# Hybrid pooling trunk on one core: in the second input phase, S4 of token block 1 formed on the chip from A12 and S2 instead of stored by the first phase and loaded

## The chip, the cores and the metric

The kernel runs on one core of a Trainium2 chip. The metric is the device time of one execution in microseconds (us), lower is better. TensorE is called PE here, VectorE DVE, ScalarE ACT, GpSimd POOL and SyncE SP, as in the profile; L783 is line 783 of the kernel.

## The reference, cut to what matters

With one layer (DEPTH = 1) only the pooling mixer runs, on 4096 tokens of width 1024, all in float32:

```python
normed = rms_norm(x, norm_w)
u, gate = split(normed @ in_w, 2)            # in_w is 1024 x 2048
pooled = trailing means of u over 2/4/8/16 tokens (one width per 256 columns) - u
mixed  = pooled @ group_w (per group of 256) + group_b
y      = mixed * scale * silu(gate)
out    = rms_norm(x + y @ out_w, final_norm_w)
```

## The kernel before, in words

**Three phases of PE work.** The group matrices are folded into the input weights at the start. Then an input phase over the first two pooling groups (kind "a"), a second input phase over the other two (kind "b", which multiplies the same normalised activations with other weights), and an output phase (kind "o"). The input phases go over four blocks of 1024 tokens (b = 0 to 3), the output phase over eight of 512. A step is one product of one block; the list `steps` has 28 + 28 + 56 of them, and the last loop of the kernel runs them in order from the third on: loads up to three steps ahead (`load_reach`, L1695), operands split one or two steps ahead (`split_reach`, L1698), the product (`run`, L1443), its eviction (`evict_in`, L1126).

**Seven products in place of eight.** Each block's activation matrix is cut into quarters A11, A12, A21, A22 (keys "11", "12", "21", "22"; each quarter is two tiles of 128 x 1024, h = 0 and 1), and multiplied in seven products P1 to P7 whose operands are sums of quarters. In the second input phase a block's products run in the order P1, P2, P6, P7, P5, P4, P3. Their operands are A11 for P1, A12 for P2, S2 = A22 - S3 for P6, S3 = A11 - A21 for P7, S1 = A11 + S2 for P5, A22 for P4, and **S4 = A12 - S2 for P3**. A11, A12, S3 and A22 come from DRAM, where the first phase left them (`sd`); S2 and S1 are formed on DVE (`form_in`, L651). S4 can either be formed on DVE (`form_s4`, L761, right after P6's operand is split, in place of A12) or be loaded. STORED (L34) says for which blocks it is stored and loaded; before, that is all four:

```python
elif q and is_stored(i, b):                                    # load_in, L645
    s["11" if i == P5 else "12"] = load_saved(b, i)
...
if i == P6 and (q or b) and not (q and is_stored(P3, b)):      # split_in, L685
    form_s4(b)
if q and is_stored({P1: P5, P2: P3}.get(i), b):                # L687
    for u in s.pop(key):
        give(u)
```

So before, A12 of a block is given back after P2's operand is split, and S4 comes in as two loads of 512 KB issued with P3's load. The first phase forms S4 in any case, for its own P3; it stores it from the ACT queue (L609) when `sd` has a place for it.

**Operands.** A product's operand is split into a high part (ACT, `copy`, L229) and the remainder (DVE, `sub`, L215) in one of four tiles op0 to op3, taken in turn; `mm3` (L778) makes three matmuls of the two parts of both sides. One step of an input phase is 48 matmuls of 128 x 512: 24 that read the first op tile, then 24 that read the second. The first matmul of an op tile reads only its high part, the second matmul reads its low part. P1, P2, P7 and P4 accumulate in banks 0 to 3, the others in banks 4 to 7; the products of one bank set follow each other as in P1, P2, then P6 on the other set, then P7, then P5 on the other, then P4, then P3 on the other.

**Slots.** Tiles of 128 x 1024 are handed out of two pools (11 `st`, 8 `vt`) by `take` (L187), the one longest free first; `give` puts a tile at the end. A tile's next writer waits for its last reader. `keep` (L1735) sets how many `vt` tiles stay reserved.

**What sets the order.** Instructions are written in program order and put on the engines' queues by a list scheduler; each engine and each DMA queue works its own queue in order. All loads and nearly all stores of the second input phase stand on SP's queue, so a transfer that waits for its tile holds back all behind it. In the middle of a block the DVE also does the pooling of the products of the block before (`pool_steps`, L1036: scans L1070, L1092, the product with the gate, and sums of four quarters stored to `sumd`, L1024), and the output weights are prepared in the same stretch (`make_wo`, L440: loads L305, scaling on ACT L320, sums on DVE, stores L340 to L345).

Of the kernel before, what the change touches and what calls it, by code (L numbers as in the profile page):

```python
# [30 lines left out]
FIRST_INNER = 1  # L31
INNER = {2: (1, 7), 4: (2, 6)}
INNER_IN = (0,)
STORED = {3: (0, 1, 2, 3)}  # L34

P1, P2, P3, P4, P5, P6, P7 = range(1, 8)
ORDER_IN = (P1, P2, P6, P7, P5, P4, P3)
# [55 lines left out]
def kernel(  # L93
# [138 lines left out]
    def split(dst, src):  # L232
# [20 lines left out]
        for i in range(P1, P7 + 1)  # L253
# [3 lines left out]
            i: [dram.tile([P, 2, H], F32, name=f"sd{b}_{i}_{h}") for h in range(2)]  # L257
            for i in (P1, P2, P7, P4, *(i for i in STORED if b in STORED[i]))
        }
# [388 lines left out]
    def is_stored(i, b):  # L648
        return b in STORED.get(i, ())

# [1245 lines left out]
```

## Time and profile before

| what | value |
|---|---|
| time, median of 3 runs | 906.63 us (905.44 to 909.16) |
| profiled execution | 905.18 us |
| its span, first to last instruction | 903.4 us |
| mean granted TensorE clock | 0.998 |
| PE busy | 895.7 us, 99% |
| DVE busy | 776.2 us, 86% |
| ACT busy | 487.6 us, 54% |
| DMA packets | 205.40 MB, mean 227 GB/s |
| chain that ended last | PE 98% |

The rows are those of the profiled execution alone; 1.8 us of its time lie outside the span. Busy PE counts overlapping matmuls, so how dense PE is has to be read from the distance between matmuls. The chain that ended last is followed back from the last instruction to what released it.

### The profile page before, as it was taken

How to read it: one execution, taken by the hardware profiler on the slowest of the kernel's cores; microseconds unless marked ns; L12 is line 12 of the kernel's file. 1: busy time of each engine (PE TensorE's matmuls, PEld its weight loads, DVE VectorE, ACT ScalarE, POOL GpSimd, SP SyncE). 2: the span in 40 equal slices, each digit the busy share in tenths (PEclk: the TensorE clock that was granted, in tenths of full speed). 3: DMA queues.
4: the chain of work that ended last, by engine and by line, in shares of the span. 5: the costliest groups of instructions: out<-in, count | busy, mean ns of one | idle time of the engine just before them, and what ended most of it. 6: DMA issues, size and time to landing. Idle time of an engine off the chain costs nothing.

```text
span 903.4 us, 12068 instructions
## 1 busy us (share of the span) xinstructions
PE 895.7 (99%) x4482; PEld 790.3 (87%) x4482; DVE 776.2 (86%) x973; ACT 487.6 (54%) x807; POOL 42.0 (5%) x75
## 2 busy tenths in 40 slices
PE   9999999999999999999999999999999999999997
PEld 7888888888888888898888888888898998999996
DVE  5999994894998998699589589799999989889897
ACT  6979547447346556355445545654446435355354
POOL 0023101101100000000000000000100000000000
PEclk9999999999999999999999999999999999999999
DMA  9986966956856844056826866855875584584652
GB/s 349 408 320 198 347 221 193 316 187 230 335 207 228 280 146 140 24 154 225 326 89 224 331 236 215 291 194 190 278 254 203 188 308 147 180 279 158 216 187 94
DMA packets 75148, 205.40 MB, mean 227 GB/s; under 512 B 6928, under 2 KB 29840, under 8 KB 75088
## 3 DMA queue, kind: packets, MB, share of 16 engines
q1 hardware_dynamic: 67440, 179.17, 56.3%
q10 hardware_dynamic: 5040, 16.79, 5.0%
q0 software_dynamic: 2608, 8.66, 2.7%
q8 instruction: 35, 0.57, 0.3%
q14 instruction: 25, 0.20, 0.1%
HBM read 130.13 MB, written 74.46 MB: 226 GB/s over the span
## 4 chain that ended last, share of the span: by engine, by line
PE 98%; DVE 1%; ACT 0%; issue 0%; DVEq 0%; ACTq 0%
PE bank L783 87%; PE bank L972 6%; PE bank L497 3%; PE bank L816 1%; PE bank L1485 0%; DVE op L215 0%; DVE w L215 0%; DVE st L215 0%; PE bank L563 0%; ACT vt L1303 0%; DVE st L1373 0%; DVE st L1345 0%; ACT vt L1335 0%; ACT vt L229 0%; DVEq L1892 0%
## 5 line engine op out<-in xcount | busy, mean ns | idle before, releaser
L783 PE MATMUL bank<-op,w 128*128 128x512 f32 x2640 | 571.4, 379 | 0.2
L783 PEld LDWEIGHTS bank<-op,w 128*128 128x128 f32 x2640 | 498.4, 189 | 72.3 <-DVE op L215 1.0
L783 PE MATMUL bank<-w,op 128*128 128x512 f32 (+1 forms) x1068 | 232.2, 377 | 0.0
L783 PEld LDWEIGHTS bank<-w,op 128*128 128x128 f32 x1068 | 198.3, 189 | 26.9 <-issue 0.2
L215 DVE TENSOR_TENSOR op<-st,op 128x1024 fp32r<-128x1024 f32 x79 | 95.2, 1209 | 28.5 <-ACT op L229 28.3
L229 ACT ACTIVATE op<-st 128x1024 fp32r<-128x1024 f32 x79 | 82.4, 1048 | 57.5 <-PE bank L783 45.0
L229 ACT ACTIVATE op<-vt 128x1024 fp32r<-128x1024 f32 x69 | 71.8, 1052 | 58.4 <-PE bank L783 32.4
L215 DVE TENSOR_TENSOR op<-vt,op 128x1024 fp32r<-128x1024 f32 x69 | 83.6, 1215 | 10.4 <-ACT op L229 10.3
L229 ACT ACTIVATE vt<-bank 128x512 f32<-128x512 f32 x94 | 53.2, 590 | 44.3 <-PE bank L783 32.5
L229 ACT ACTIVATE bank<-bank 128x512 f32<-128x512 f32 (+1 forms) x76 | 38.0, 502 | 63.4 <-PE bank L783 32.1
L215 DVE TENSOR_TENSOR op<-s_st,op 128x1024 fp32r<-128x1024 f32 x31 | 37.6, 1217 | 12.0 <-ACT op L229 12.0
L229 ACT ACTIVATE op<-s_st 128x1024 fp32r<-128x1024 f32 x31 | 32.4, 1049 | 21.9 <-PE bank L783 11.8
L1373 DVE TENSOR_TENSOR vt<-bank,vt 128x512 f32<-128x512 f32 x56 | 37.9, 680 | 3.3 <-PE bank L783 3.3
L972 PE MATMUL bank<-w,op 128*128 128x256 f32 x288 | 40.0, 275 | 0.0
L972 PEld LDWEIGHTS bank<-w,op 128*128 128x128 f32 x288 | 37.8, 192 | 1.3
L215 DVE TENSOR_TENSOR vt<-bank,vt 128x512 f32<-128x512 f32 x50 | 32.7, 683 | 6.9 <-PE bank L783 6.8
L1237 POOL TENSOR_SCALAR oms<-oss 128x2 f32<-128x2 f32 x14 | 9.8, 696 | 615.4 <-ACT st L1264 443.2
L1070 DVE TENSOR_TENSOR_SCAN vt<-vt,bf 128x512 f32<-128x512 f32 x28 | 34.4, 1267 | 1.3 <-ACT vt L229 1.3
L215 DVE TENSOR_TENSOR w<-st,w 128x1024 fp32r<-128x1024 f32 (+2 forms) x25 | 28.1, 1132 | 8.5 <-ACT w L229 8.5
L229 ACT ACTIVATE w<-st 128x1024 fp32r<-128x1024 f32 (+2 forms) x25 | 24.2, 984 | 18.8 <-DMA st<-wod 9.0
L215 DVE TENSOR_TENSOR vt<-vt,vt 128x1024 f32<-128x1024 f32 (+1 forms) x29 | 33.0, 1140 | 0.1
L229 ACT ACTIVATE st<-bank 128x512 f32<-128x512 f32 x34 | 20.0, 594 | 24.0 <-PE bank L783 16.2
(171 smaller groups left out, 817.9 us busy)
## 6 DMA issues: line engine op xcount, KB each, us to landing
st<-in_x SPq DMA_DIRECT2D x27, 512.0 KB, 5.8
st<-in_xt SPq DMA_DIRECT2D x27, 512.0 KB, 8.9
vt<-in_x SPq DMA_DIRECT2D x27, 512.0 KB, 5.0
sd<-st ACTq DMA_DIRECT2D x27, 512.0 KB, 5.6
vt<-yd SPq DMA_DIRECT2D x18, 512.0 KB, 5.6
st<-sd SPq DMA_DIRECT2D x17, 512.0 KB, 5.4
out<-vt SPq DMA_DIRECT2D x17, 512.0 KB, 3.5
yd<-st SPq DMA_DIRECT2D x16, 512.0 KB, 2.9
```

The costliest lines, as they stand in the source:

```text
L215: made.append(nc.vector.tensor_tensor(out=dst, in0=a, in1=b, op=op))
L229: made.append(nc.scalar.activation(dst, src, func, **how))
L497: latest[0] = nc.tensor.matmul(ps2[kk][:, j * 256 : (j + 1) * 256], a[:, kk, 2 * j + t, :], maps if len(pairs) == 1 else woven(maps), star ...
L783: latest[0] = nc.tensor.matmul(ps, a, b, start=start and n == 0, stop=stop and n == 2, skip_group_check=True).ins
L816: latest[0] = nc.tensor.matmul(quarter_bank(banks_[c], n), a[:, x_, k, c * P : (c + 1) * P], right[:, y_, k], start=start and k + m == 0, ...
L972: latest[0] = nc.tensor.matmul(dst, a[k][x_], b[k][y_], start=start and k + n == 0, stop=k == 1 and n == 2, skip_group_check=True,).ins
L1070: nc.vector.tensor_tensor_scan(s[:, j, at:end], v[:, j, at:end], v[:, j, at - win : end - win], sums_of[j] if sums_of else 0.0, ALU.add, A ...
L1237: nc.gpsimd.tensor_scalar(out=ms, in0=ss, scalar1=-0.5 / D, scalar2=-0.5 * EPS, op0=ALU.mult, op1=ALU.add)
L1373: partial["added"] = nc.vector.tensor_tensor(out=dst, in0=src, in1=dst, op=ALU.add).ins
```

## The change

```diff
-STORED = {3: (0, 1, 2, 3)}
+STORED = {3: (0, 2, 3)}
```

`STORED` has one key, 3, which is P3. Block 1 leaves the list, and three things follow in the program. The first phase has no place in `sd` for block 1's S4, so two stores on the ACT queue go. The second phase issues no load for it, so two loads on SP's queue go. And A12 of block 1 (in tiles vt6 and st2) isn't given back after P2; `form_s4` subtracts S2 from it in place, two DVE instructions, and P3's operand is split from there. As A12's tiles stay taken and the two tiles of the load aren't taken, the tiles that later instructions get are others from there on, and the scheduler's order changes around it. All other instructions are the same, and PE's order is the same row for row. Names in the rows below: st, vt and s_st tiles are slots (st9_98 is slot st9; s9_st1_3058 is slot st1 in its second life, and its last number differs between the two programs only by counting), bank4_73 is bank 4.

**DVE, where block 1's S2 is formed** (S2 in s9_st1 for h = 0 and s10_st7 for h = 1; st9 and st5 hold A11 and become S1; op2 and op3 are P6's operand; op rows are the low parts). Before:

```order
L215 TENSOR_TENSOR s9_st1_3058<-vt7_107,s7_st3_3022 128x1024
L215 TENSOR_TENSOR st9_98<-s9_st1_3058,st9_98 128x1024
L215 TENSOR_TENSOR s10_st7_3059<-vt1_101,s8_st10_3023 128x1024
L215 TENSOR_TENSOR op2_87<-s9_st1_3058,op2_87 128x1024
L215 TENSOR_TENSOR st5_94<-s10_st7_3059,st5_94 128x1024
L215 TENSOR_TENSOR op3_88<-s10_st7_3059,op3_88 128x1024
```

Now:

```order
L215 TENSOR_TENSOR s9_st1_3054<-vt7_107,s7_st3_3018 128x1024
L215 TENSOR_TENSOR vt6_106<-vt6_106,s9_st1_3054 128x1024
L215 TENSOR_TENSOR st9_98<-s9_st1_3054,st9_98 128x1024
L215 TENSOR_TENSOR s10_st7_3055<-vt1_101,s8_st10_3019 128x1024
L215 TENSOR_TENSOR op2_87<-s9_st1_3054,op2_87 128x1024
L215 TENSOR_TENSOR st2_91<-st2_91,s10_st7_3055 128x1024
L215 TENSOR_TENSOR op3_88<-s10_st7_3055,op3_88 128x1024
```

The rows on vt6 and st2 are the new S4. The second of them stands where S1's second half (st5) stood; that row has moved on, to the next place.

**DVE, ahead of P7's operand of block 1** (op0 and op1; st0 and s11_st4 belong to the pooling and its sums). Before:

```order
L215 TENSOR_TENSOR st0_89<-vt3_103,st0_89 128x1024
L215 TENSOR_TENSOR op0_85<-s7_st3_3022,op0_85 128x1024
L215 TENSOR_TENSOR vt2_102<-st6_95,st0_89 128x512
L215 TENSOR_TENSOR op1_86<-s8_st10_3023,op1_86 128x1024
L215 TENSOR_TENSOR vt2_102<-vt2_102,st6_95 128x512
L215 TENSOR_TENSOR s11_st4_3060<-st0_89,vt2_102 128x512
L215 TENSOR_TENSOR op2_87<-st9_98,op2_87 128x1024
```

Now:

```order
L215 TENSOR_TENSOR st0_89<-vt3_103,st0_89 128x1024
L215 TENSOR_TENSOR st5_94<-s10_st7_3055,st5_94 128x1024
L215 TENSOR_TENSOR vt2_102<-st6_95,st0_89 128x512
L215 TENSOR_TENSOR op0_85<-s7_st3_3018,op0_85 128x1024
L215 TENSOR_TENSOR vt2_102<-vt2_102,st6_95 128x512
L215 TENSOR_TENSOR op1_86<-s8_st10_3019,op1_86 128x1024
L215 TENSOR_TENSOR s11_st4_3056<-st0_89,vt2_102 128x512
L215 TENSOR_TENSOR op2_87<-st9_98,op2_87 128x1024
```

Between st0 and op0 there now stand two rows, st5 of 128 x 1024 and the first vt2 of 128 x 512; before, op0 followed st0 directly.

**ACT, evictions of P2 and P6 of block 1** (from banks 0 to 3 and 4 to 7; the L320 rows scale output weights after their loads; op rows are high parts). Before:

```order
L229 ACTIVATE op2_87<-st9_98 128x1024
L229 ACTIVATE vt4_104<-bank4_73 128x512
L229 ACTIVATE vt4_104<-bank5_74 128x512
L320 ACTIVATE s7_st3_3022<-s7_st3_3022,colt_114 128x512 x2
L229 ACTIVATE vt0_100<-bank6_75 128x512
L229 ACTIVATE vt0_100<-bank7_76 128x512
L229 ACTIVATE op3_88<-st5_94 128x1024
```

Now:

```order
L229 ACTIVATE op2_87<-st9_98 128x1024
L320 ACTIVATE s10_st7_3055<-s10_st7_3055,colt_114 128x512 x2
L229 ACTIVATE st6_95<-bank6_75 128x512
L320 ACTIVATE s7_st3_3018<-s7_st3_3018,colt_114 128x512
L229 ACTIVATE st6_95<-bank7_76 128x512
L229 ACTIVATE op3_88<-st5_94 128x1024
L320 ACTIVATE s7_st3_3018<-s7_st3_3018,colt_114 128x512
L229 ACTIVATE s11_st4_3056<-bank4_73 128x512
L229 ACTIVATE s11_st4_3056<-bank5_74 128x512
```

Banks 4 and 5 of P6 are now evicted last of the four, behind two loads' scaling, and into s11_st4, which the pooling's sums leave only when their store to `sumd` has landed; before, they went into vt4, first.

## Prediction

> **What bounds the kernel now.** I read the page's first two parts, then the engines' busy time by stage, then the chain that ended last.
>
> ```profile
> PE 895.7 (99%) x4482; PEld 790.3 (87%) x4482; DVE 776.2 (86%) x973; ACT 487.6 (54%) x807; POOL 42.0 (5%) x75
> ```
>
> By itself 99% says little, since matmuls overlap. The table by stage (time, then PE, weight loads, DVE, ACT, POOL, clock, DMA share, GB/s) and one row of the chain say more:
>
> ```profile
> 60.00:394.00 334.00, 334.00 (x1589) 293.57 (x1588) 281.07 (x306) 194.09 (x297) 24.81 (x43) 1.00 0.61 215
> 394.00:571.00 177.00, 176.98 (x823) 154.71 (x822) 147.17 (x159) 87.95 (x169) 0.00 (x0) 1.00 0.65 236
> 571.00:894.00 323.00, 323.00 (x1741) 289.77 (x1742) 295.51 (x436) 156.53 (x260) 9.75 (x14) 1.00 0.61 210
> ```
>
> ```profile
> 394.49 176.34 PE bank L783 x817
> ```
>
> From 60 to 894 us PE is idle for 0.02 us in all, and 817 matmuls follow each other every 176.34/817 = 0.216 us at a granted clock of 1.00. So PE sets the end, and what the change can take from the time is nothing: it leaves PE's matmuls and their order alone, and there is no wait of PE to shorten in the stretch that it touches. It can only add, by making an operand or a bank late. The question is which cushions it eats.
>
> The Trainium skill ("Perfetto Trace Analysis", section "Identifying the Most-Contended Engine") says that matmul busy time is a poor measure of how near a kernel is to its limit, and that weight-load busy time should be read; by its 87% some 113 us of PE would still be open. The row of 0.216 us speaks against that here: the skill's "TensorE: Matmul & The Clock Gate", Part 1, gives 215.7 ns between matmuls of 512 columns at full clock, which the trace agrees with. By the one rule a removed wait could pay, by the row it can't; I go by the row, and what is left for the other is in the chance of the faster rival.
>
> **What goes.** In the first phase two stores of S4 leave ACT's queue, in the second two loads leave SP's. The first two rows are those stores; of the second two, the first holds one of those loads beside one for block 2, the second is the other load.
>
> ```profile
> 160.72 0.33 ACTq L609 DMA_DIRECT2D sd<-st  x1
> ...
> 162.47 0.33 ACTq L609 DMA_DIRECT2D sd<-st  x1
> ```
>
> ```profile
> 427.76 1.97 SPq L626 DMA_DIRECT2D st<-sd  x2
> ...
> 431.66 0.32 SPq L626 DMA_DIRECT2D s_st<-sd  x1
> ```
>
> That is 2 x 0.33 us of issuing on ACT at 161 to 163 us, some 1.3 us on SP, and four transfers of 0.52 MB out of 205 MB. PE hides them all: it is busy for 334.00 of 334 us around the stores and did not wait for S4's loads either. I cost them at 0. If PE did not cover them, the removed issues would be worth 0.7 us on ACT and 1.3 us on SP at the most.
>
> **What comes.** Two DVE subtractions of 128 x 1024. DVE around block 1's P6 and P7 (start, duration, form; a bracket is idle time ahead and its releaser):
>
> ```profile
> 404.69 1.22 DVE L215 TENSOR_TENSOR s_st<-vt,s_st 128x1024 f32<-128x1024 f32 x1
> 405.94 1.23 DVE L215 TENSOR_TENSOR st<-s_st,st 128x1024 f32<-128x1024 f32 x1
> 408.69 1.23 DVE L215 TENSOR_TENSOR s_st<-vt,s_st 128x1024 f32<-128x1024 f32 x1 [1.52 <-DMA vt<-sd]
> 409.83 1.22 DVE L215 TENSOR_TENSOR op<-s_st,op 128x1024 fp32r<-128x1024 f32 x1
> 410.96 1.22 DVE L215 TENSOR_TENSOR st<-s_st,st 128x1024 f32<-128x1024 f32 x1
> 412.10 1.22 DVE L215 TENSOR_TENSOR op<-s_st,op 128x1024 fp32r<-128x1024 f32 x1
> 413.23 3.63 DVE L1070 TENSOR_TENSOR_SCAN vt<-vt,bf 128x512 f32<-128x512 f32 x3
> ...
> 421.95 1.21 DVE L215 TENSOR_TENSOR st<-vt,st 128x1024 f32<-128x1024 f32 x1
> 423.08 1.21 DVE L215 TENSOR_TENSOR op<-s_st,op 128x1024 fp32r<-128x1024 f32 x1
> 424.22 0.68 DVE L215 TENSOR_TENSOR vt<-st,st 128x512 f32<-128x512 f32 x1
> 424.82 1.21 DVE L215 TENSOR_TENSOR op<-s_st,op 128x1024 fp32r<-128x1024 f32 x1
> 425.96 0.68 DVE L215 TENSOR_TENSOR vt<-vt,st 128x512 f32<-128x512 f32 x1
> 426.67 0.69 DVE L215 TENSOR_TENSOR s_st<-st,vt 128x512 f32<-128x512 f32 x1
> ```
>
> Starts in a dense run lie 1.14 us apart after a row of 1024 and 0.60 after one of 512, since neighbours overlap by 0.08. The first subtraction (vt6) falls behind the row at 404.69, into the idle 1.52 us that waits for A22's second load: it costs 1.14 to 1.25 us of DVE and nothing of the time. If that load landed earlier, the cover would shrink, but then everything behind it would start earlier by as much.
>
> The second (st2) takes the place of S1's second half (the row at 410.96), so everything from 412.10 to 421.95 stays where it is. S1's half is what moves: with the first vt2 row it now stands ahead of op0's low part. **The term of the sum** is there: op0 moves from 423.08 to 423.08 + 1.14 + 0.60 = 424.82, and is done at 424.82 + 1.21 = 426.03 in place of 424.29.
>
> When does PE want it? P1 of block 1 starts at 394.33, and P1, P2 and P6 are 144 matmuls:
>
> ```profile
> 394.33 31.25 PE L783 MATMUL bank<-op,w 128*128 128x512 f32 x144
> ```
>
> 144 x 0.2158 = 31.08, so P7's first matmul starts at 425.41, and its second, the first to read the low part, at 425.63. Before, op0 was ready 1.34 us ahead of that. Now it is 0.40 late, and with 0.05 us for the wait's end (0.02 to 0.1 lie between releases and starts in these rows) **PE stands still for about 0.45 us**. It is dense afterwards, so the end moves by that. Bounds: 0 if A22's load lands 0.4 us earlier, since the first subtraction leaves the DVE free at 408.30; 1.3 + 0.45 if the scheduling around st0 slips by another row of 1024 (estimate from the rows above).
>
> Queued behind op0 on DVE are op1, done at 424.82 + 1.14 + 0.60 + 1.21 = 427.77 while PE wants its low part at 425.63 + 24 x 0.2158 = 430.81, and P5's op2, done near 429.5 and wanted at 435.99. Both have 3 us and more left, and S1's moved half is wanted later still, as P5's second operand at 441. P3's operand no longer waits for a load: S4 is there from 412 us, wanted at 456.
>
> **The evictions** change more than the DVE. ACT, and SP with landing times in this stretch (KB, median us from issue to landing):
>
> ```profile
> 421.93 0.59 ACT L229 ACTIVATE vt<-bank 128x512 f32<-128x512 f32 x1
> ...
> 428.04 1.33 ACT L320 ACTIVATE s_st<-s_st,colt 128x512 f32<-128x512 f32 x2 [4.42 <-DMA s_st<-in_out_w]
> 429.28 1.06 ACT L229 ACTIVATE vt<-bank 128x512 f32<-128x512 f32 x2
> 430.23 1.05 ACT L229 ACTIVATE op<-st 128x1024 fp32r<-128x1024 f32 x1
> ```
>
> ```profile
> s_st<-in_out_w SPq DMA_DIRECT2D x4, 512.0 KB, 3.7
> st<-sd SPq DMA_DIRECT2D x4, 512.0 KB, 6.1
> ...
> sumd<-s_st SPq DMA_DIRECT2D x1, 512.0 KB, 4.3
> ```
>
> Bank 4, which P5 overwrites, was evicted at 421.93. Now ACT first needs the weight load into s10, which waits for S1's moved half: issued 424.3, landed 424.3 + 3.7 = 428.0, scaled by 429.3, bank 6 by 429.8. The load into s7 follows op0: 426.03 + 3.7 = 429.7, first scaling 430.5, bank 7 431.0, op3 432.0, second scaling 432.6. Bank 4 goes into s11, whose store is issued after DVE's sum: op1 done 427.77, sum 428.4, store landed 428.4 + 4.3 = 432.7. So bank 4 is out at 433.3. P5 starts at 394.33 + 192 x 0.2158 + 0.45 = 436.2. The cushion falls from 13.3 to 2.9 us and holds; I cost it at 0. With 6.1 us for each of these transfers, the longest median above, bank 4 is out at 435.7, still in time.
>
> Farther on, block 2's P2 and P6 keep their DVE work in another order, with their low parts no later than before, and from block 3 on the rows stand in the same order as before, but for single rows of 512 or 1024 with over 3 us left. Cost 0.
>
> **Sum:** 905.18 (profiled) + 0.45 = 905.63 for the profiled execution. That execution lies 1.45 us under the median of the runs, 906.63, so the median after should be **907.1 us**.
>
> **The rivals.**
> - Hidden altogether: A22's load, which fixes the dense run on DVE, lands 0.4 us earlier, and op0 is in time. The loads ahead of it on SP are the same, which speaks against it. 906.6.
> - Faster: 2.1 MB less on the DMA queues and two loads fewer in front of block 2's take a wait away. PE's 0.02 us of idle time in 834 speaks against any gain; 906.6 at best, and over 0.5% less only if the runs scatter.
> - Slower, by the late eviction of bank 4: ACT stands in line behind the load into s10, issued 11 us later than before, so each us by which that landing passes 3.7 + 2.9 = 6.6 us holds P5 up by one. At twice the longest median, 12.2 us, P5 would wait 5.6 us and the kernel would take 907.1 + 5.6 = 912.7. Against it: medians of 3.7 for these loads, and two fewer loads beside them.
>
> On that rival the Trainium skill ("TensorE: Matmul & The Clock Gate", section on HAM oscillation) adds that a PE gap over about 3.4 us halves the clock for the next window. A gap of 5.6 us would then cost about 1.7 us more (an estimate from that page's window), 914.4, one of 0.45 us nothing; no row between 60 and 894 us shows such a gap, and the clock there is 1.00.
>
> - That the change does not do what it says is excluded by the order: the two rows are there, the four transfers are not.
>
> **How the numbers follow.** The forecast has a chance of 0.75, hidden 0.12, the late eviction 0.10 (over 0.5% in 0.04), faster 0.03. About 0.5%, 4.5 us, is what a measurement of this kernel can tell from no change. So faster 0.02, within 0.92, slower 0.06 (the two hundredths beyond the eviction are scatter). The three runs of before lie from 1.2 under to 2.5 over their median. The range takes the hidden case less that scatter, 905.4, and the forecast plus it, 909.6; an eviction late by up to 2.5 us falls within it.
>
> **What would show it.** In the profile after: DVE's idle time ahead of S2's second half down from 1.52 to under 0.5 us; op0's low part near 426.0; a PE wait for DVE's op of 0.4 to 0.5 us near 425.6; bank 4's eviction near 433 and no wait of PE for ACT there; 203.3 MB in place of 205.4. A PE wait for an eviction near 436, or a second one in block 2, would make the prediction wrong.

## The result, and the profile after

| | before | after |
|---|---|---|
| median of 14 runs each | 905.46 us (904.90 to 909.16) | 909.22 us (905.96 to 911.70) |
| ratio after to before, 95% interval | | 1.0029 (1.0018 to 1.0040) |
| profiled execution | 905.18 us | 910.07 us |
| its span | 903.4 us | 908.3 us |
| DMA packets | 205.40 MB | 203.30 MB |

The medians lie 3.76 us apart; by the ratio the change costs about 2.6 us (0.0029 x 905.46). That is within the bound of 0.5% and within the range given, but the sum had only 0.45 us. The runs of after come in lumps: four of 14 lie between 905.96 and 906.19, within 0.3 us of what the forecast's one term gives on this median (905.46 + 0.45); the other ten lie at 907.45 and above. So the question is what the others pay for.

Two stages of the profile after, to be read against the table quoted in the prediction (the first stage, 60 to 394 us, is full as before; time, PE, weight loads, DVE, ACT, POOL, clock, DMA share, GB/s):

```profile
394.00:571.00 177.00, 176.43 (x820) 154.21 (x819) 146.96 (x156) 86.27 (x166) 0.00 (x0) 1.00 0.62 224
571.00:894.00 323.00, 320.32 (x1720) 286.79 (x1719) 295.47 (x429) 155.47 (x257) 9.58 (x14) 0.99 0.62 213
```

Before, PE was idle for 0.02 us between 60 and 894. Now it is idle for 0.57 in the middle stretch and 2.68 in the last, where the clock also reads 0.99. Each stretch has a single gap. PE's rows of the profile after, with the idle time ahead and its releaser:

```profile
426.26 6.09 PE L783 MATMUL bank<-op,w 128*128 128x512 f32 x27 [0.57 <-DVE op L215]
...
574.25 9.08 PE L783 MATMUL bank<-op,w 128*128 128x512 f32 x33 [2.68 <-DVE op L215]
```

The first is the wait that was forecast, ahead of P7 of block 1. The second is ahead of P7 of **block 3**, two blocks behind the last instruction that the change adds. Finer stretches of the same table, directly behind the second gap:

```profile
574.30:575.50 1.20, 1.20 (x4) 0.97 (x5) 1.20 (x2) 0.00 (x0) 0.00 (x0) 0.60 0.99 314
575.50:579.00 3.50, 3.50 (x12) 2.87 (x11) 1.57 (x2) 0.00 (x0) 0.00 (x0) 0.65 0.97 315
```

PE ran there at a granted clock below 1.00 and lost 0.40 x 1.20 + 0.35 x 3.50 = 1.7 us, as much as 3.4 us at half speed would. The two gaps and this loss, 0.57 + 2.68 + 1.7 = 4.95, account for the span's 4.9 us.

DVE's rows of after that answer to those of the prediction, and two of block 3:

```profile
408.85 1.23 DVE L215 TENSOR_TENSOR s_st<-vt,s_st 128x1024 f32<-128x1024 f32 x1 [0.66 <-DMA vt<-sd]
...
424.99 1.22 DVE L215 TENSOR_TENSOR op<-s_st,op 128x1024 fp32r<-128x1024 f32 x1
...
550.95 1.22 DVE L215 TENSOR_TENSOR s_st<-s_st,vt 128x1024 f32<-128x1024 f32 x1
...
572.98 1.22 DVE L215 TENSOR_TENSOR op<-vt,op 128x1024 fp32r<-128x1024 f32 x1
```

The first two are S2's second half of block 1 and op0's low part, done at 426.21 where 426.03 was forecast. The last two are the same two instructions in block 3. Before, they stood here:

```profile
549.32 1.22 DVE L215 TENSOR_TENSOR st<-s_st,s_st 128x1024 f32<-128x1024 f32 x1
...
569.58 1.22 DVE L215 TENSOR_TENSOR op<-s_st,op 128x1024 fp32r<-128x1024 f32 x1
```

They are 1.63 and 3.40 us later in after, while PE by itself would be 0.57 later. PE had nothing to spare there even before. These are its weight load for P7's second matmul in block 3, the first to read that operand's low part, and then the matmul ahead of it and that matmul:

```profile
570.85 0.19 PEld L783 LDWEIGHTS bank<-op,w 128*128 128x128 f32 x1 [0.42 <-DVE op L215]
```

```profile
570.45 0.38 PE L783 MATMUL bank<-op,w 128*128 128x512 f32 x1
570.85 0.48 PE L783 MATMUL bank<-op,w 128*128 128x512 f32 x1
```

The two start 0.40 us apart and not 0.216, so PE had already lost 0.18 us. A matmul's row lasts 0.38 us, so a delay of up to 0.38 - 0.216 = 0.16 us leaves no idle time; what is left of this one is the 0.02 us that the prediction quotes as PE's whole idle time. The row of the chain quoted there, 394.49 with 176.34 us, ends at 570.83, at this place.

Why the two rows are later shows in the chain of work that ended last. Before it was 98% PE; in after it leaves PE at 494.98 and comes back to it at 574.25 (start, duration, what):

```profile
494.98 0.52 ACT s_st L229
495.50 6.13 DMA s_st<-in_out_w
...
504.45 1.24 DVE op L215
505.70 3.96 DMA s_st<-in_out_w
...
520.78 4.90 DMA s_st<-wod
...
549.08 7.19 DMA st<-wod
...
573.06 1.15 DVE op L215
```

This is a **side chain** of 79 us beside PE: the output weights of `make_wo` are loaded (L305), scaled, summed, stored and loaded again, and DVE does the pooling and P7's operand behind them in order. SP's rows of before for its stations:

```profile
497.93 0.38 SPq L305 DMA_DIRECT2D s_st<-in_out_w  x1
498.40 0.86 SPq L305 DMA_DIRECT2D st<-in_out_w  x2
...
517.74 0.44 SPq L428 DMA_DIRECT2D s_st<-wod  x1
...
545.30 0.32 SPq L1024 DMA_DIRECT2D sumd<-st  x1
...
547.46 0.38 SPq L451 DMA_DIRECT2D st<-wod  x1
```

Before, the last of block 2's weight loads was issued by 499.26, and the reload at 517.74. In after the last load gets a tile that op1's subtraction reads until 505.69, so it is issued at 505.70, the reload at 520.78, and the load at 549.08 instead of 547.46. The question for the experiments was what makes this chain late: the two DVE rows, the other tiles, or the transfers themselves.

### The profile page after: what moved, and what is told of

It is laid out like the page before. It is cut to its first block, busy times and chain, and to the rows that moved or that the text cites. A ratio compares the mean times of both kernels' runs of the same rounds, so it can differ in the third digit from the quotient of the medians.

```text
span 908.3 us, 12064 instructions
## 1 busy us (share of the span) xinstructions
PE 897.3 (99%) x4482; PEld 791.3 (87%) x4482; DVE 779.7 (86%) x975; ACT 487.5 (54%) x807; POOL 41.8 (5%) x75
## 2 busy tenths in 40 slices
DMA packets 74572, 203.30 MB, mean 224 GB/s; under 512 B 6864, under 2 KB 29776, under 8 KB 74512
## 4 chain that ended last, share of the span: by engine, by line
PE 87%; DVE 7%; DMA 3%; issue 2%; ACT 1%; SPq 0%; DVEq 0%; ACTq 0%
PE bank L783 77%; PE bank L972 6%; PE bank L497 3%; DVE vt L1070 2%; DVE op L215 1%; DVE st L215 1%; DMA s_st<-in_out_w 1%; PE bank L816 1%; DVE s_st L215 1%; DMA st<-wod 1%; DVE vt L1092 1%; DMA s_st<-wod 1%; DVE w L215 1%; DMA early<-in_wut 0%; DVE vt L215 0%
## 5 line engine op out<-in xcount | busy, mean ns | idle before, releaser
L229 ACT ACTIVATE op<-vt 128x1024 fp32r<-128x1024 f32 x71 | 73.9, 1052 | 57.8 <-PE bank L783 31.9
L215 DVE TENSOR_TENSOR op<-vt,op 128x1024 fp32r<-128x1024 f32 x71 | 86.0, 1217 | 11.4 <-ACT op L229 11.3
L229 ACT ACTIVATE vt<-bank 128x512 f32<-128x512 f32 x90 | 50.7, 592 | 41.9 <-PE bank L783 27.7
L1373 DVE TENSOR_TENSOR vt<-bank,vt 128x512 f32<-128x512 f32 x56 | 37.9, 681 | 3.0 <-PE bank L783 3.0
L215 DVE TENSOR_TENSOR st<-st,vt 128x1024 f32<-128x1024 f32 (+1 forms) x29 | 33.9, 1200 | 3.9 <-DMA st<-sd 3.8
L215 DVE TENSOR_TENSOR vt<-bank,vt 128x512 f32<-128x512 f32 x46 | 30.1, 683 | 6.0 <-PE bank L783 6.0
```

Of the source, the lines that this page charges most:

```text
L215: made.append(nc.vector.tensor_tensor(out=dst, in0=a, in1=b, op=op))
L229: made.append(nc.scalar.activation(dst, src, func, **how))
L1373: partial["added"] = nc.vector.tensor_tensor(out=dst, in0=src, in1=dst, op=ALU.add).ins
```

## The experiments

In every run below, "waits" are PE's in the profiled execution, which is one execution among those of the median, and ratios are to the kernel before on the same chip, with 95% intervals.

**x0: the changed kernel once more**, without an edit.

> The changed kernel once more, for a second profile and as the base of its neighbours. Its first profile shows two waits of PE, 0.57 us ahead of P7 of block 1 and 2.7 us ahead of P7 of block 3. Slot theory (the second wait comes from a weight load of block 2 that got a tile which is freed late): the wait at 571 to 575 us is there again, 1 to 3 us long, and the kernel takes 2 to 3.5 us more than before. Landing theory (the second wait is one transfer that happened to land 2 us late, 7.2 us in place of 5.2): the wait is mostly gone in this profile, at most 1 us, and the time is within 1 us of before.

Measured: 908.82 us, 1.0032 (1.0014 to 1.0050). The profiled execution (912.36, span 910.6, among the four slowest of 12) had one wait, at another place than expected:

```profile
558.60 24.65 PE L783 MATMUL bank<-op,w 128*128 128x512 f32 x101 [4.21 <-ACT bank L229]
```

Here DVE, then ACT, ahead of it:

```profile
555.69 1.23 DVE L215 TENSOR_TENSOR s_st<-s_st,vt 128x1024 f32<-128x1024 f32 x1 [1.18 <-DMA sumd<-s_st]
```

```profile
557.01 1.06 ACT L229 ACTIVATE op<-s_st 128x1024 fp32r<-128x1024 f32 x1 [3.02 <-DVE s_st L215]
557.97 0.58 ACT L229 ACTIVATE bank<-bank 128x512 f32<-128x512 f32 x1
```

S2's second half waits until the store to `sumd` has left its tile; ACT's copy of P6's operand waits for S2; and the eviction of the bank that PE needs next stands behind that copy on ACT, though its own data are ready. PE starts 0.05 us after the eviction. In before this eviction had room:

```profile
551.60 0.58 ACT L229 ACTIVATE bank<-bank 128x512 f32<-128x512 f32 x1
```

It was done at 552.18, some 1.4 us ahead of need (before's P2 reaches that bank at about 553.6, counting matmuls from its dense row). So lateness shows at two exits: at the bank when S2 is well over 1.4 us late, at P7's operand otherwise, or at both. The wait ahead of P7 of block 1 was absent in this execution: PE had reached P1 0.5 us later (394.84), so op0 was in time.

**x1: the DVE work alone.** Before, with two DVE rows that change no value where S4 would be formed; stores, loads and tiles as before.

```diff
+        if i == P6 and q and b == 1:
+            for u in s["22"]:
+                on_vector(u, u, u, ALU.max)
```

> The kernel before, with all four blocks' S4 stored and loaded, and two more rows of 128x1024 on DVE at the place where the change forms S4 (each takes the maximum of a tile of A22 with itself, so nothing of the result changes). Slots and transfers are those of before. Slot theory: only the first wait comes, 0.4 to 0.6 us ahead of P7 of block 1, and none of over 0.3 us ahead of P7 of block 3; 0.5 us over before. Theory that the work on DVE is behind all of it: both waits come, 2.5 to 3.5 us over before.

Measured: 912.77 us, 1.0065 (1.0043 to 1.0087), more than the whole change. PE's rows, then SP's:

```profile
425.79 54.40 PE L786 MATMUL bank<-op,w 128*128 128x512 f32 x250 [0.26 <-DVE op L215]
...
558.23 22.07 PE L786 MATMUL bank<-op,w 128*128 128x512 f32 x88 [4.02 <-ACT bank L229]
```

```profile
434.31 0.32 SPq L626 DMA_DIRECT2D s_st<-sd  x1
434.69 0.42 SPq L305 DMA_DIRECT2D s_st<-in_out_w  x1
...
501.33 0.38 SPq L305 DMA_DIRECT2D s_st<-in_out_w  x1
```

The last weight load of block 1 stands behind S4's load on SP and is issued at 434.69; before, it was issued at 432.08, and in after, where S4's load is gone, at 429.53. Block 2's weight loads start at 501.33 instead of before's 497.93, with before's tiles. So two DVE rows in block 1 suffice for the late chain, and the other tiles aren't needed: the theory that put all of it down to the tile of the last load falls. In after, with S4's loads gone and other tiles, about 3 us of this come back (1.0065 against x0's 1.0032 beside it, though the intervals overlap).

The two rows don't act by their length alone. As in the change, S1's second half moves behind them, and with it the weight load of block 1 that goes into the tile of S2's second half: before, it was the second of two at 411.07, and now it goes out with the next one, near 424 us:

```profile
411.07 2.60 SPq L305 DMA_DIRECT2D s_st<-in_out_w  x2
```

```profile
424.02 2.07 SPq L305 DMA_DIRECT2D s_st<-in_out_w  x2
```

The first row is of before, the second of x1; after's is at 424.49. The prediction has this load, 11 us late, but follows it to bank 4 alone and not to the weights that it brings.

**x2: the other tiles and the removed transfers alone.** After, without the two subtractions.

```diff
-        if i == P6 and (q or b) and not (q and is_stored(P3, b)):
+        if i == P6 and (q or b) and not (q and is_stored(P3, b)) and not (q and b == 1):
```

> The changed kernel without the two subtractions on DVE: block 1's P3 multiplies A12 where S4 belongs, which is left out. Tiles, loads and stores are those of the changed kernel. Slot theory: no wait ahead of P7 of block 1, and the wait ahead of P7 of block 3 is there, 1 to 3 us; 1.5 to 3 us over before. Theory that the work on DVE is behind all of it: neither wait, the time of before within 0.3 us.

Measured: 906.14 us, 1.0007 (0.9992 to 1.0022). PE's wait in block 3:

```profile
572.41 3.94 PE L783 MATMUL bank<-op,w 128*128 128x512 f32 x17 [1.11 <-DVE op L215]
```

S2 starts at 550.87, as late as in after's profile (550.95) and 1.55 us behind before's, without the two DVE rows. That the tiles do this by themselves isn't shown by one execution, since after's and x0's lie 4.7 us apart with one program. The wait is 1.11 and not 2.68 since the weight load issued at 549.00 let ACT go on at 554.12, where after's landed at 556.27. Most of the time isn't lost without the DVE rows. The first two weight loads of block 1 stand at 411.28 here, as in before; the one that waits until 424.49 in after isn't late.

**x3: the last weight load into another pool,** which frees it from op1's subtraction (after, `load_rows` with a pool to choose; tiles handed out later change with it).

```diff
-                us[kh, n] = load_rows(out_w, 4 * kh + 2 * h, n * H)
+                us[kh, n] = load_rows(out_w, 4 * kh + 2 * h, n * H, vt if h and kh and n else None)
```

> The changed kernel with one tile changed: the fourth weight load of block 2 (the one issued at 505.7 us, behind DVE's split into op1) gets a tile of the vt pool, which is free by 500 us. Slot theory: the load is issued near 500.5 us, the sums of the output weights stand some 3 us earlier on DVE, the wait ahead of P7 of block 3 falls under 0.5 us, and only the first wait stays, 0.6 us: 0.5 to 1 us over before. Theory that the work on DVE, or a transfer that lands late by itself, is behind the second wait: it stays at 1 to 3 us.

Measured: 908.52 us, 1.0024 (1.0010 to 1.0037), no clear gain. The load was issued 4.0 us earlier than in after (501.68 against 505.70), but it landed no earlier: ACT could begin to scale it at 510.33, in after at 509.68. ACT in after, then SP, ACT and PE in x3:

```profile
509.68 0.72 ACT L320 ACTIVATE s_st<-s_st,colt 128x512 f32<-128x512 f32 x1 [3.10 <-DMA s_st<-in_out_w]
```

```profile
501.68 0.42 SPq L305 DMA_DIRECT2D vt<-in_out_w  x1
```

```profile
510.33 1.33 ACT L320 ACTIVATE vt<-vt,colt 128x512 f32<-128x512 f32 x2 [3.83 <-DMA vt<-in_out_w]
```

```profile
556.71 17.32 PE L783 MATMUL bank<-op,w 128*128 128x512 f32 x79 [1.31 <-ACT bank L229]
575.34 2.86 PE L783 MATMUL bank<-op,w 128*128 128x512 f32 x12 [1.31 <-DVE op L215]
```

Both exits show in one execution.

**y1 and y2: the side chain one step earlier.** If the whole chain is late and nothing else, starting block 2's output weights with P7 instead of P5 should take the waits away in after (y1) and do nothing for before (y2).

```diff
-            if kind == "b" and b in (1, 2) and i == P5:
+            if kind == "b" and (b, i) in ((1, P5), (2, P7)):
                 make_wo(b - 1)
```

> The changed kernel, with the preparation of the output weights in block 2 asked for one step earlier (behind P7 in place of P5). Late-chain theory (the work beside PE, output weights by way of DRAM and pooling, reaches block 3 late, and PE waits there for what is late by more than before): the chain starts some us earlier, PE waits under 0.5 us in block 3, and only the wait ahead of P7 of block 1 stays; 0.5 to 1 us over before, little scatter. Theory that block 3's own transfers are to blame, whenever the chain starts: waits of 1 to 4 us in block 3 as in the changed kernel, 2.5 to 4 us over before.

> The kernel before with the same edit alone. Late-chain theory: no wait of PE in block 3, 0 to 0.5 us under before, less scatter above the median. Theory that block 3's own transfers are to blame: as before, or slower by the disturbed order.

Measured: y1 905.26 us, 0.9993 (0.9983 to 1.0004); y2 905.10 us, 0.9997 (0.9985 to 1.0008). In y1 PE's wait in block 1 is still there, and behind it nothing; the stretch from 571 is full again and its clock 1.00:

```profile
425.96 150.27 PE L783 MATMUL bank<-op,w 128*128 128x512 f32 x695 [0.46 <-DVE op L215]
```

```profile
571.00:894.00 323.00, 323.00 (x1742) 289.75 (x1741) 295.07 (x435) 156.67 (x261) 9.03 (x14) 1.00 0.61 209
```

```profile
512.95 0.72 SPq L428 DMA_DIRECT2D s_st<-wod  x1
```

The reload is issued at 512.95 instead of after's 520.78, and S2 starts at 548.86, ahead of before's 549.32. One line that asks for the side chain earlier takes away the loss; the tiles and the order of rows around it on DVE, ACT and SP change with it, and PE's order doesn't. It brings nothing clear beyond before (y2), where PE is the bound and was dense.

**y3 and y4: S4's second half behind P7's operand on DVE,** to take away the wait of block 1 by itself (y4: with y1's line as well).

```diff
+            if kind == "b" and u is xs[b]["12"][1]:
+                put_off.append((u, s2))
...
+        if put_off and i == P6:
+            with tc.issue_after(latest_split[0]):
+                u, s2 = put_off.pop()
+                sub(u, u, s2)
```

> The changed kernel with the second half of S4's subtraction put behind the operand of P7 on DVE, so that S1's second half stands again where it stood before. Late-chain theory: no wait ahead of P7 of block 1, the first weight load of block 1 is not delayed, and block 3 loses about what the kernel without the two subtractions lost there, 0 to 1.2 us; 0 to 1.2 us over before. Theory that the tiles alone make block 3 late: no first wait, but 2 to 4 us in block 3.

> Both edits on the changed kernel: S4's second half behind P7's operand, and the output weights of block 2 asked for one step earlier. Late-chain theory: no wait of PE of over 0.3 us between 60 and 894 us, the time of before or up to 0.5 us less. Theory that block 3's own transfers are to blame: waits of 1 us and more in block 3, 1 to 4 us over before.

Measured: y3 910.73 us, 1.0044 (1.0027 to 1.0062), where the late-chain theory had at most 1.2 us over before; y4 906.16 us, 1.0000 (0.9987 to 1.0013). In y3 the wait of block 1 is gone, but the put-off row keeps S2's tile, into which one of block 1's weight loads goes, until 428.11; that load is now the last of the three instead of the first. Block 2's reload is issued at 523.91, 3.1 us later than in after, and PE pays in block 3:

```profile
557.87 22.46 PE L786 MATMUL bank<-op,w 128*128 128x512 f32 x95 [4.11 <-ACT bank L229]
```

So taking away the wait of block 1 gained nothing. Whether it made block 3's wait longer isn't shown, since x0 has 4.21 us there without it, and which landing carried it was not separated. In y4, with the chain started earlier, the wait in block 3 is 0.75 us, where at most 0.3 was expected.

**z1 to z4: a dose of DVE work in block 2 of before,** two or four rows that change no value, ahead of P4's sums (z1, z2) or behind them (z3, z4):

```diff
         elif i == P4:
...
+            if q and b == 2:
+                for u in ev["21"] * 2:
+                    on_vector(u, u, u, ALU.max)
```

> The kernel before with two rows of 128x1024 more on DVE (maximum of a tile with itself, nothing of the result changes), not in block 1 but near 527 us, ahead of the sums of P4 of block 2; order, tiles and transfers are else those of before, row for row. They make the chain beside PE late by 2.3 us. Late-chain theory: DVE passes it on undiminished, and PE, which has no cushion ahead of P7 of block 3, waits 1.8 to 2.3 us in block 3; 2 to 2.5 us over before, or 3.5 to 4 if the gap halves the clock for a window, as the gap of 2.7 us did in the changed kernel. Theory that tiles and transfers are to blame: no change, under 0.5 us.

> The same with four rows, 4.6 us. Late-chain theory: PE waits 3.9 to 4.6 us in block 3, at bank 3's eviction ahead of P2 or ahead of P7; with two windows at half clock, as after the gaps of 4.1 and 4.2 us, 6 to 7.5 us over before. Theory that tiles and transfers are to blame: no change, under 0.5 us.

> The kernel before with two rows of 128x1024 more on DVE (maximum of a tile with itself), now tied behind the sums of P4 of block 2, so that they can't move forward into DVE's idle time near 496 us. Some 0.9 us of idle time stands behind them on DVE, so the chain beside PE gets 1.3 to 2.3 us late from 530 us on. Late-chain theory (what is late on DVE from 530 us on reaches P7 of block 3 undiminished, and PE has no cushion there): PE waits 1 to 2.3 us in block 3, 1 to 2.5 us over before. Theory that it takes late transfers, and late DVE work alone is caught up: under 0.4 us of waits in block 3, no change.

> The same with four rows; the scheduler also puts some rows of ACT and SP in block 3 in another order. The chain is 3 to 4.6 us late. Late-chain theory: PE waits 2.5 to 4.6 us in block 3, the clock is halved for a window or two, 4 to 7 us over before. Theory that it takes late transfers: under 0.5 us of waits, no change.

Measured: z1 906.02 us, 0.9994 (0.9983 to 1.0005), and z2 905.95, 0.9996 (0.9986 to 1.0007): no dose was given, because the scheduler put the rows into idle time of DVE near 496 to 501 us, so these two say nothing on it. Their profiles show a wait of 1.12 and of 0.94 us ahead of P7 of block 3 all the same, and the medians no loss. Whether executions of before have such waits too, its one profile can't say. z3 911.03, 1.0052 (1.0036 to 1.0069), and z4 912.37, 1.0065 (1.0049 to 1.0080). S2's row in z3, then SP's, then PE's (z4's waits are in the table below):

```profile
553.92 1.23 DVE L215 TENSOR_TENSOR st<-s_st,s_st 128x1024 f32<-128x1024 f32 x1 [3.44 <-DMA sumd<-st]
```

```profile
545.05 2.06 SPq L451 DMA_DIRECT2D st<-wod  x2
547.39 0.32 SPq L1024 DMA_DIRECT2D sumd<-st  x1
```

```profile
556.84 19.44 PE L783 MATMUL bank<-op,w 128*128 128x512 f32 x81 [3.29 <-ACT bank L229]
```

Lateness made in block 2 comes out at the same exits, without any of the change. That DVE work alone makes it isn't shown. In z3 the DVE row ahead of S2's second half is 1.08 us late (549.26 instead of 548.18), and then S2 waits 3.44 us for the store to `sumd`, which in this program stands behind two weight loads on SP (547.39 instead of 545.30). z4 has the same order there. So the theory that it takes late transfers stands beside the other.

Put in order by S2's second half in block 3, the profiled executions read as follows. The medians are those of each kernel's own runs, on several chips; before's lie between 905.46 and 905.88 there.

| kernel | S2 starts | waits of PE in block 3 | median |
|---|---|---|---|
| y1 | 548.86 | none | 905.26 |
| y2 | 549.23 | none | 905.10 |
| before | 549.32 | none | 905.46 |
| y4 | 550.17 | 0.75 | 906.16 |
| z1 | 550.25 | 1.12 | 906.02 |
| z2 | 550.46 | 0.94 | 905.95 |
| x2 | 550.87 | 1.11 | 906.14 |
| after | 550.95 | 2.68 | 909.22 |
| x3 | 553.80 | 1.31 + 1.31 | 908.52 |
| z3 | 553.92 | 3.29 | 911.03 |
| y3 | 554.96 | 4.11 | 910.73 |
| x1 | 555.32 | 4.02 | 912.77 |
| x0 (as after) | 555.69 | 4.21 | 908.82 |
| z4 | 558.43 | 4.27 + 1.53 | 912.37 |

## Why the prediction was right in kind and short in size

- **PE as the bound, and that the change can only add: held.** No version was faster than before beyond its interval, not even y1 with the late chain removed.
- **The range held by luck.** The sum had 0.45 us; the median of after, 909.22, is below the range's end of 909.6 because that end holds 2.5 us of scatter of before's runs, not because the second wait was in it.
- **The term of the sum, P7 of block 1: held.** 0.57 us of idle time against 0.45, op0 ready at 426.21 against 426.03. By matmul starts the delay is 0.74 us: PE arrived 0.11 us earlier than in before, op0 was 0.18 us later than forecast, and a delay's first 0.16 us leave no idle time. (The upper bound for a further row of 1024, 1.3 + 0.45, is 1.14 + 0.45 by the prediction's own spacing.) It hangs, as said, on A22's landing against PE's arrival: 0.46 in y1, 0.26 in x1, 0.91 in x3, none in x0. DVE's idle time ahead of S2 fell from 1.52 to 0.66, which is not the "under 0.5" that was named.
- **Bank 4's eviction, the slower rival: rightly put aside.** PE did not wait for it. ACT's row in after:

```profile
434.43 1.09 ACT L229 ACTIVATE s_st<-bank 128x512 f32<-128x512 f32 x2 [0.16 <-DMA sumd<-s_st]
```

It starts at 434.43 with bank 4 and is done with both banks at 435.52; 433.3 was forecast for bank 4, P5's need 436.2.
- **The stores and loads that go, costed at 0: in doubt for the side chain.** With them still there, the DVE work by itself cost 1.0065 (x1) against 1.0032 (x0), and S4's loads stand ahead of a weight load on SP. But x1 and x0 differ in tiles too, and their intervals overlap.
- **The step that failed: "Farther on ... Cost 0."** It went by the order of rows and took the cushions of the single rows that changed places to be over 3 us. No wait of PE was traced to those. It left out rows that kept their place and only moved in time: P7's operand of block 3 was ready at 569.58 + 1.22 = 570.80 in before, 0.13 us after PE could have taken it (570.45 + 0.216 = 570.67), and its weight load had waited 0.42 us for it; the bank's eviction had 1.4 us. The other "Cost 0" that let this through is in the evictions: the weight load that goes out 11 us late was followed to bank 4 and no farther. The term that was mis-sized is this one: 0 was written, 2.68 us of wait in after's profile and 4.21 in x0's were measured, and on top 1.7 and 2.6 us of half clock. The sentence on what would make the prediction wrong named a second wait in block 2; it came in block 3.
- **On the clock,** the prediction took from the Trainium skill ("TensorE: Matmul & The Clock Gate", section on HAM oscillation) that a gap of over about 3.4 us halves the clock for a window. The mechanism and the window's 3.4 us agree with after's rows; the gap here was shorter, 2.68 us. By the measured row the loss is 1.7 us; by the page's figure it would have been none.

Shown: the loss is paid at two exits in block 3; starting block 2's output weights earlier takes it away (y1), the two DVE rows, with the rows that move behind them, bring it about with before's tiles (x1), and without them most of it is gone (x2). The way from block 1's late load through block 2 is read from the chain and from SP's rows, and no run cuts it at one place alone. That the removed loads give part of it back rests on x1 beside x0 and on SP's rows, not on a run that removes the loads alone. Open: how after's lumps divide. Its two profiled executions differ by 4.7 us at S2 with the same program, so landing times decide much, but which transfer does it in which run was not separated; before, too, has single runs up to 909.16 us that no profile here explains. Why x2, as late at S2 as after's profile, is 2.7 us faster in the median than x0 beside it also stays open: its weight load of block 1 isn't late, but its reload in block 2 is issued at 520.91, no earlier than after's.

## What to carry to other kernels

A dense bound engine hides how thin the cushions of its side chains are: before costing a moved row at nothing, follow its chain of tiles, loads and stores to the next place where the bound engine takes something from it, however many steps later, and read the cushion there, by the wait of its weight load and the distance of its matmuls and not by idle time. Look there too for an in-order queue in which a ready eviction stands behind a copy that waits. Where such a chain is late, try to start it one step earlier: here one line took away what the late rows cost.

## What the runs showed of the hardware

- The clock was cut after short gaps: PE gaps of 2.68 us (after) and more show it, gaps of up to 1.53 us (z4) don't. How much is lost doesn't follow from the length alone. These rows are from the start of the gap on, of x0 (a gap of 4.21 us), then of y3 (4.11):

```profile
554.40:558.60 4.20, 0.00 (x0) 0.00 (x0) 2.99 (x4) 1.59 (x3) 0.00 (x0) 0.81 0.50 151
558.60:562.00 3.40, 3.40 (x8) 2.77 (x9) 3.40 (x4) 2.81 (x9) 0.00 (x0) 0.50 0.15 29
562.00:565.50 3.50, 3.50 (x13) 2.87 (x13) 3.50 (x4) 1.55 (x5) 0.00 (x0) 0.73 0.87 269
```

```profile
553.70:557.80 4.10, 0.06 (x1) 0.00 (x0) 3.66 (x4) 1.76 (x3) 0.00 (x0) 1.00 0.64 221
...
558.50:562.00 3.50, 3.50 (x10) 2.79 (x9) 3.50 (x5) 2.42 (x9) 0.00 (x0) 0.51 0.30 95
```

In x0 the clock fell while PE still waited, and PE lost 0.50 x 3.40 + 0.27 x 3.50 = 2.6 us behind the gap, so that wait cost nearly 7. In y3 it was 1.00 through the wait and fell only after PE had gone on; PE lost 0.49 x 3.50 = 1.7 us. The expectation of z2 counts two windows after a gap of 4.1 us; y3 shows one.
- A load that is issued earlier need not land earlier: in x3 one of 512 KB was issued 4.0 us ahead of after's, and the scaling behind it began 0.65 us later.
